# Attention maps and output rows of a two-layer decoder turned by transposing transfers instead of TensorE

## The chip, the cores and the metric

The kernel runs on one core of a Trainium2 chip. TensorE multiplies matrices, VectorE and ScalarE work on whole tiles, GpSimd does a few small steps, and SyncE issues most of the transfers; ScalarE issues some too. The metric is the device time of one execution in microseconds (us), the median over several runs. A profile comes from one execution taken by the hardware profiler.

## The reference

A sequence of 512 tokens, with 16 learned meta tokens put ahead of it, goes through two layers at width 1024. The first is gated linear attention. The second is differential softmax attention, and it is the one that matters here:

```python
proj = xn @ w_in                                  # 1024 x 8192
q, k, v, z = jnp.split(proj, 4, axis=-1)          # 8 heads; q and k have two halves p of 128
s = jnp.einsum('bhpqd,bhpkd->bhpqk', qb, kh) * scale + bias[None, :, None]
s = jnp.where(dist >= 0, s, -jnp.inf)
p = jax.nn.softmax(s, axis=-1)
a = p[:, :, 0] - lam * p[:, :, 1]                 # the map of a head
o = jnp.einsum('bhqk,bhkv->bhqv', a, vh)          # v has 256 columns a head
o = head_rms(o) * gnorm * (1.0 - lambda_init)
y = jax.nn.silu(z) * o
h = h + y @ w_out                                 # 2048 x 1024
```

All of it is fp32. A head has 4 blocks of 128 queries; block b sees the meta tokens and b + 1 blocks of 128 keys. At the end comes an RMS norm of the 512 rows.

## The kernel before, in words

Every fp32 operand of a product is split into a high part, rounded to TensorE's fast fp32 format, and a low remainder (`split`: ScalarE writes the high part, L276, VectorE the low one, L277). A product is then three passes, high by high, high by low, low by high (`mm3`, L400; `product`, L431, inside a Strassen-like scheme with seven products called `Unit`; `project`, L421). Weights come in pieces of 1 MB into two buffers called `raw`, by SyncE (L285 and L298), and are split just ahead of their use: `a11`, `a12`, `a22`, `sum` and `wh`/`wl` are the operands that a `Unit` makes of a piece.

The order of TensorE is written out by hand (a manual schedule). ScalarE, VectorE, GpSimd and SyncE get theirs from a scheduler that goes by priorities and its own estimates of durations; a function marked `urgent` gets a higher priority. Transposing transfers keep the order in which the program issues them. All engines run their lists strictly in order.

A planner, the `Weaver`, lays the list of TensorE. It holds a queue of generators, which are the projections of the next head (`q_diff_z`, `q_diff_v`, `q_diff_k`, `q_diff_q`) and the output projections of earlier heads (`q_diff_out2`). `fill(us)` takes products from the queue for so many microseconds; `finish` empties it, `follow` sets a step to be laid after so many microseconds of filling, and `land` lays all such steps at once. `behind` holds steps that are issued on SyncE just after the next load of weights.

A head of the second layer has four steps for each block, from block 3 down to block 0, laid between stretches of filling (`diff_steps`, L1663):

- A, `scores`: the products of q and k (on TensorE, L400 into `ps`), the bias added and the minimum found by VectorE (L1680), the exponentials by ScalarE (L1682), and the map a from both halves by VectorE (L1685 to L1687).
- B, `turn`: TensorE turns the map, one 128x128 transpose for each block of keys (L1695) and one for the last 32 columns, where the meta tokens are (L1696). ScalarE and VectorE split it from PSUM into `aT` and `am`.
- C, `values`: the products of the turned map and v (L400, L1711). ScalarE takes the squares (L1716), GpSimd the power -1/2 (L1718), and ScalarE copies the scaled rows to `on` (L1719).
- E, `rows`: TensorE turns `on` with two transposes (L1725), VectorE multiplies by the gate z into `yt` (L1728), and the two splits go to the output operand `hT`.

The steps of a head are laid as A3 A2 B3 A1 C3 B2 E3 A0 C2 B1 E2 C1 B0 E1 C0 E0 (the digit is the block). After A0, SyncE loads the next head's bias tile `T` (`bias_tile`, L1543), for which VectorE must have read the old one.

v of heads 1 to 6 is already turned by transfers (`turn_by_dma`): ScalarE copies the two 16-bit halves of each word apart (`planes`, L589), sends them to device memory (`vd`, L590), SyncE brings them back with transposing transfers (L598, and L600 for the last 128 columns, `lands`), and `landed` splits the result (L575, L576).

The output projection of a pair of heads (0 and 1, 2 and 3, 4 and 5) is laid as a whole among the steps of heads 2, 4 and 6; its sums are added into `hacc`. Heads 6 and 7 are projected at the end (`final_rows`).

## Time and profile before

| | us |
|---|---|
| median of 3 runs | 972.53 (971.72 to 973.37) |
| span of the profiled execution | 970.2 |
| TensorE busy | 957.1 (99%) |
| VectorE busy | 778.4 (80%) |
| ScalarE busy | 628.0 (65%) |
| GpSimd busy | 50.6 (5%) |
| DMA traffic | 104.94 MB in 128521 packets, mean 108 GB/s |

The profiled execution is 2.3 us shorter than the median. The heads of the second layer run from about 500 to 940 us of the span. In rows of the timeline the columns are start, length, engine, line, operation, the tile written and the tiles read, and the shape; in brackets stands the idle time before it and what ended it. A row with x4 stands for four instructions. "SPq" and "ACTq" are the issues of transfers by SyncE and ScalarE: their length is how long the issue holds the queue, not how long the data travels. In rows that group instructions, the total busy time is followed by the mean of one in ns, and then by the idle time before them.

### The profile page before, as it was taken

What the parts mean: (1) busy time and instruction counts of PE and PEld (TensorE: products, weight loads), DVE (VectorE), ACT (ScalarE), POOL (GpSimd) and SP (SyncE); (2) the same over time, 40 slices, a digit from 0 to 9 for tenths busy, and PEclk for the clock granted to TensorE, in tenths of its full rate; (3) what the DMA queues carried; (4) which work ended last, traced back from release to release, by engine and by line L of the source; (5) the groups of instructions that cost most, each with busy time, mean ns of one, the idle gap of its engine ahead of it and who ended that gap; (6) DMA issues with size and microseconds to landing.
All of it is one profiled execution on the core that took longest, in us unless ns stands there. A gap on an engine that the chain in (4) does not pass through costs nothing. (4 is left out here: it accounts for less than half of the span.)

```text
span 970.2 us, 18065 instructions
## 1 busy us (share of the span) xinstructions
PE 957.1 (99%) x6993; PEld 906.5 (93%) x6993; DVE 778.4 (80%) x1586; ACT 628.0 (65%) x1304; POOL 50.6 (5%) x68
## 2 busy tenths in 40 slices
PE   8999999999999999999999999999999999999997
PEld 8999999999999999898899998898998999989996
DVE  7989885886888887568997985977958879677785
ACT  7776755577647567656757774576764677655583
POOL 1000000000000100000001001001010000000001
PEclk9999999999999999999999999999999999999999
DMA  7322223635363245224355525135252352412212
GB/s 197 88 86 60 79 81 122 148 99 129 120 156 96 79 121 154 62 92 151 100 132 147 131 78 153 51 97 140 86 148 88 99 138 86 148 61 84 87 66 87
DMA packets 128521, 104.94 MB, mean 108 GB/s; under 512 B 51101, under 2 KB 112829, under 8 KB 128432
## 3 DMA queue, kind: packets, MB, share of 16 engines
q1 hardware_dynamic: 123104, 93.80, 35.1%
q10 hardware_dynamic: 5328, 9.95, 2.8%
q8 instruction: 56, 0.92, 0.4%
q14 instruction: 33, 0.27, 0.1%
HBM read 83.64 MB, written 11.80 MB: 98 GB/s over the span
## 5 line engine op out<-in xcount | busy, mean ns | idle before, releaser
L277 DVE TENSOR_TENSOR wl<-raw,wh 128x1024 fp32r<-128x1024 f32 x98 | 119.5, 1222 | 24.8 <-ACT wh L276 16.8
L276 ACT ACTIVATE wh<-raw 128x1024 fp32r<-128x1024 f32 x98 | 103.2, 1055 | 52.6 <-PE by L968 23.2
L431 PE MATMUL bv<-x,wh 128*128 128x264 f32 (+1 forms) x656 | 97.6, 286 | 0.0
L431 PE MATMUL bx<-x,wh 128*128 128x264 f32 (+1 forms) x640 | 94.9, 286 | 0.7 <-ACT u L452 0.6
L431 PEld LDWEIGHTS bv<-x,wh 128*128 128x128 f32 x656 | 86.5, 188 | 0.6 <-DVE z L479 0.3
L431 PEld LDWEIGHTS bx<-x,wh 128*128 128x128 f32 x640 | 84.5, 188 | 1.9 <-ACT u L452 1.2
L452 ACT ACTIVATE u<-bx 128x264 f32<-128x264 f32 (+1 forms) x120 | 45.4, 380 | 32.3 <-PE bx L431 31.1
L421 PE MATMUL bx<-x,wh 128*128 128x512 f32 (+1 forms) x256 | 62.4, 386 | 0.0
L277 DVE TENSOR_TENSOR wl<-sum,wh 128x1024 fp32r<-128x1024 f32 x41 | 50.1, 1221 | 14.3 <-ACT wh L276 13.9
L431 PE MATMUL bv<-x,wl 128*128 128x264 f32 (+1 forms) x328 | 55.2, 285 | 0.1
L1718 POOL TENSOR_TENSOR st<-st,mhalf 128x1 f32<-128x1 f32 x32 | 31.0, 970 | 464.4 <-ACT on L1716 408.9
L431 PE MATMUL bx<-x,wl 128*128 128x264 f32 (+1 forms) x320 | 53.9, 285 | 0.0
L1682 ACT ACTIVATE p<-p,st 128x528 f32<-128x528 f32 (+3 forms) x64 | 36.5, 571 | 25.4 <-DVE st L1680 24.9
L421 PEld LDWEIGHTS bx<-x,wh 128*128 128x128 f32 x256 | 44.5, 188 | 7.9
L276 ACT ACTIVATE wh<-sum 128x1024 fp32r<-128x1024 f32 x41 | 43.3, 1056 | 13.0 <-PE bv L431 4.0
L431 PE MATMUL by<-x,a12h 128*128 128x264 f32 (+1 forms) x320 | 46.5, 285 | 0.2 <-ACT t L1646 0.2
L431 PE MATMUL bx<-x,a11h 128*128 128x264 f32 (+1 forms) x320 | 46.3, 285 | 0.0
L431 PEld LDWEIGHTS bv<-x,wl 128*128 128x128 f32 x328 | 45.9, 188 | 0.4 <-issue 0.3
L431 PEld LDWEIGHTS bx<-x,wl 128*128 128x128 f32 x320 | 45.2, 188 | 0.6 <-DVE wl L277 0.2
L276 ACT ACTIVATE a11h<-raw 128x512 fp32r<-128x512 f32 x41 | 25.7, 627 | 28.6 <-DMA raw<-in_diff_w_in_dram 14.2
L431 PEld LDWEIGHTS bx<-x,a11h 128*128 128x128 f32 x320 | 42.2, 188 | 0.7
L431 PEld LDWEIGHTS by<-x,a12h 128*128 128x128 f32 x320 | 41.8, 188 | 0.4 <-ACT t L1646 0.4
(475 smaller groups left out, 2632.2 us busy)
## 6 DMA issues: line engine op xcount, KB each, us to landing
raw<-in_gla_w_in_dram SPq DMA_DIRECT2D x48, 512.0 KB, 4.5
raw<-in_diff_w_in_dram SPq DMA_DIRECT2D x42, 512.0 KB, 4.8
raw<-in_diff_w_in_dram SPq DMA_DIRECT2D x11, 1024.0 KB, 6.3
raw<-in_gla_w_out_dram SPq DMA_DIRECT2D x8, 1024.0 KB, 5.7
raw<-in_diff_w_out_dram SPq DMA_DIRECT2D x8, 1024.0 KB, 6.4
vd<-planes ACTq DMA_DIRECT2D x12, 268.0 KB, 7.1
vd<-keep ACTq DMA_DIRECT2D x12, 264.0 KB, 2.3
T<-bdr SPq DMA_DIRECT2D x8, 264.0 KB, 5.0
```

Of the source, the lines that this page charges most:

```text
L276: act.activation(hi, src, AF.Copy)
L277: dve.tensor_tensor(lo, src, hi.bitcast(F32), op=ALU.subtract)
L421: pe.matmul(bank, a[:, k, :], b[k] if n0 is None else b[k][:, n0 + i * nn:n0 + (i + 1) * nn], start=n == 0 and ks[0] == 0, stop=n == len(t ...
L431: pe.matmul(bank[:, :x[q].shape[2]], w[p][:, k * P:(k + 1) * P], x[q][:, k, :], start=first and i == 0, stop=i == len(PASSES) - 1, skip_gr ...
L452: W.moved = act.activation(t, self.bx[:, :self.n], AF.Copy, scale=self.sc)
L1682: act.activation(p[:, :nk], p[:, :nk], AF.Exp, scale=-1.0, bias=st[:, m:m + 1], accum_out=st[:, 2 + m:3 + m])
L1718: pool.tensor_tensor(ms, ms, mhalf[:, :1], op=ALU.pow)
```

## The change

The maps of heads 0 to 6, all four blocks, are turned by transfers: ScalarE copies the 16-bit halves of the map apart (L1704 of the new kernel) and sends them to device memory (`ad`, L1706); SyncE brings them back with two transposing transfers a block, one for the blocks of keys into `p0` to `p3` and one for the last 128 columns into `e1` to `e3`, or `keep` for block 0 (L1716); `landed` splits them into `aT` (L575). Head 7 keeps the transposes on TensorE.

The output rows of heads 2 to 6 go the same way, once for the whole head: ScalarE copies each block's `on` apart into `yt` (L1757) and sends it to `ye` (L1760); after the last block one transposing transfer brings all four back (L1765), VectorE multiplies by z in one instruction (L1770), and one split of 1024 columns follows. Heads 0, 1 and 7 keep `rows` on TensorE (L1783).

The steps of heads 0 to 6 become A3 A2 A1 A0 B3 C3 B2 E3 C2 B1 E2 C1 B0 E1 C0 E0, with 4 us of filling after each A. The two halves of an output projection are spread: one of the pair 0 and 1 to head 2, the other to head 3, then one to head 4 and one to head 5 for the next pair, and both of the third pair in head 6. The filling is divided by new shares. Steps carry tags, and `land` is called for one tag where its result is needed: "v", "y" with the head, "a" with the block. The transposing transfers of v are issued directly and no longer behind a load of weights. `tri` and `hacc` move to other pools.

Counted over the whole program, TensorE loses 138 transposes (80 to 10 of L1695, 32 to 4 of L1696, 64 to 24 of L1725) and keeps all other products. ScalarE gains 28 copies of maps, 20 copies of rows and 48 issues; SyncE gains 61 transposing transfers, 28 and 28 for the maps and 5 for the rows.

```diff
@@ turn_by_dma
-                W.follow((4.0, turn if direct else lambda: behind.append((turn, None))))
+                W.follow((4.0 if tag is None else 9.0, turn if direct else lambda: behind.append((turn, tag))), tag=tag)
@@ gate
         if s.z is None:
+            W.land(("y", heads.index(s) - 2))
@@ turned_back2: last
             split3(s.vm, pm, 32, short[:, NM + 1:NM + 2])
+            for back, take, tag in pending:
+                W.follow((0.1, back), (9.0, take), tag=tag)
+            pending.clear()
@@ turned_back2
             if m:
+                W.land("y")
                 s.leave = turn_by_dma(T(ep, [P, 2, 536], F32, "planes", bufs=1),
-                                      [(slice(3, 1, -1), 0), (slice(1, None, -1), 272)], 240, 0.0 if heads.index(s) % 2 else 11.0, done, last)
+                                      [(slice(3, 1, -1), 0), (slice(1, None, -1), 272)], 240, 9.0, done, last, True, "v")
@@ diff_steps: scores
+        by_pe, rows_by_pe = hd == D_HEADS - 1, hd in (0, 1, D_HEADS - 1)
...
+            if by_pe:
+                act.activation(r.p, r.a, AF.Copy)
+            else:
+                pl = words(r.p).rearrange("p (h c) -> p h c", h=2)
+                act.activation(pl, words(r.a).rearrange("p (c h) -> p h c", h=2), AF.Copy)
+                r.dr = T(dp, [P, 2, L], U16, "ad", bufs=4)
+                act.dma_start(r.dr[:, :, :nk], pl)
+                W.follow((9.0, lambda: back(r)), tag=("a", b))
             return r
+
+        def back(r):
+
+            w = (r.b + 1) * P
+            rows = r.dr.rearrange("p h c -> (p h) c")
+            r.ends = (T(ep, [P, P], F32, f"e{r.b}", bufs=1) if r.b else keep2[:, 4 * D:]).rearrange("p (j c) -> p j c", c=P)
+            for o, c0, c1 in ((r.p[:, :w].rearrange("p (j c) -> p j c", c=P), 0, w), (r.ends, r.nk - P, r.nk)):
+                tc.keep_in_program_order(sp.dma_start(words(o), rows[:, c0:c1], transpose=True))
@@ diff_steps: turn
+            if not by_pe:
+                W.land(("a", r.b))
...
+            else:
+                landed(hi, lo, r.p[:, :w], ticked())
+                with tc.issue_after(W.split.ins):
+                    split3(r.am, r.ends[96:, 0, :], 64)
@@ diff_steps: values
             act.activation(r.on, po, AF.Copy, scale=ms)
+            if not rows_by_pe:
+                pl = words(T(ep, [P, 256], F32, "yt", bufs=1)).rearrange("p (h c) -> p h c", h=2)
+                act.activation(pl, words(r.on).rearrange("p (c h) -> p h c", h=2), AF.Copy)
+                if s.rows is None:
+                    s.rows = T(dp, [4, P, 2, 256], U16, "ye", bufs=3)
+                act.dma_start(s.rows[b], pl)
+
+        def rows_back():
+
+            s.y = T(ep, [P, 2, NR], F32, "planes", bufs=1)
+            tc.keep_in_program_order(sp.dma_start(words(s.y), s.rows.rearrange("b p h c -> (b p h) c"), transpose=True))
+
+        @urgent
+        def rows_landed():
+            with tc.issue_after(W.mark.ins):
+                dve.tensor_tensor(s.y, s.y, s.z, op=ALU.mult)
+            split(*ys[hd], s.y)
@@ the loop over heads
+        if hd in (2, 3, 5):
+            q_diff_out2(pair, ys[pair:pair + 2], [hd % 2])
+        if hd == D_HEADS - 2:
+            q_diff_out2(pair, ys[pair:pair + 2], range(2))
...
+        if hd == 4:
+            q_diff_out2(pair, ys[pair:pair + 2], [0])
...
-        steps = [(A, 0), (A, 1), (B, 0), (A, 2), (C, 0), (B, 1), (E, 0), (A, 3), (C, 1), (B, 2), (E, 1), (C, 2), (B, 3),
-                 (E, 2), (C, 3), (E, 3)]
+            steps = [(A, 0), (A, 1), (A, 2), (A, 3), (B, 0), (C, 0), (B, 1), (E, 0), (C, 1), (B, 2), (E, 1), (C, 2), (B, 3), (E, 2), (C, 3), (E, 3)]
...
-        share = {A: 1.5, B: 1.1, C: 1.1, E: 0.5}
+        share = {A: 1.5, B: 1.1, C: 1.1, E: 0.5} if last else {B: 1.6, C: 1.0, E: 0.3 if hd < 2 else 0.0}
+        W.land("v")
```

The change moves instructions on every engine. Three places are shown. In each row stand the line, the operation, the tile written and the tiles read (a number in a name is a running one), and the shape.

SyncE in head 0, from the load of the next bias tile T. Before:

```order
L1543 DMA T_9437<-bdr_1019 128x528
L298 DMA raw_9683<-in_diff_w_in_dram 128x4x256 x2
L598 DMA_TRANSPOSE planes_9383<-vd_9384 128x2x512 x2
L600 DMA_TRANSPOSE lands_9688<-vd_9384 128x1x512
L298 DMA raw_9690<-in_diff_w_in_dram 128x4x256 x2
L298 DMA raw_9718<-in_diff_w_in_dram 128x4x256 x2
```

Now (the names with `ad` are the map's halves in device memory):

```order
L1549 DMA T_9342<-bdr_1019 128x528
L1716 DMA_TRANSPOSE p_1600_9145<-ad_9163 128x3x256
L1716 DMA_TRANSPOSE e_1644_9350<-ad_9163 128x1x256
L1716 DMA_TRANSPOSE p_1617_9237<-ad_9255 128x2x256
L1716 DMA_TRANSPOSE e_1657_9424<-ad_9255 128x1x256
L1716 DMA_TRANSPOSE p_1638_9322<-ad_9340 128x1x256
L1716 DMA_TRANSPOSE keep_8187<-ad_9340 128x1x256
L298 DMA raw_9705<-in_diff_w_in_dram 128x4x256 x2
L605 DMA_TRANSPOSE planes_9373<-vd_9374 128x2x512 x2
L607 DMA_TRANSPOSE lands_9591<-vd_9374 128x1x512
```

Six transposing transfers of the head's maps now stand between T and the next load of weights, and v's transposes have moved behind the first of these loads.

ScalarE in head 0, where the first split of the weights loaded behind T stands (a11h). `ps` is a bank of PSUM with a block's values, `on` the scaled rows (L1716 and L1719 before, L1751 and L1754 now), `am` the meta columns of a map, `u` a partial sum of a `Unit`. Before, with block 2's rows:

```order
L1715 ACTIVATE ps_9466<-st_9125 128x1
L1716 ACTIVATE on_9477,st_9125<-ps_9466 128x257
L1719 ACTIVATE on_9477<-ps_9466,st_9125 128x256
L452 ACTIVATE u_9498<-bx_9339 128x264
L276 ACTIVATE aT_1675_9524<-ps_9518 128x256
L407 ACTIVATE am_9523<-ps_9519 32x128
L408 ACTIVATE am_9523<-ps_9519 32x128
L276 ACTIVATE a11h_9693<-raw_9683 128x512
```

Now, with block 3's rows:

```order
L408 ACTIVATE am_9408<-e_1624_9266 32x128
L276 ACTIVATE wh_9461<-raw_9209 128x1024
L276 ACTIVATE a11h_9711<-raw_9705 128x512
L575 ACTIVATE aT_1665_9478<-p_1600_9145,tick_9480 128x384
L1750 ACTIVATE ps_9442<-st_9059 128x1
L407 ACTIVATE am_9477<-e_1644_9350 32x128
L1751 ACTIVATE on_9456,st_9059<-ps_9442 128x257
L408 ACTIVATE am_9477<-e_1644_9350 32x128
L1754 ACTIVATE on_9456<-ps_9442,st_9059 128x256
```

The split a11h stood behind the rows of block 2; now it stands ahead of the split of block 2's map and of both steps of `on` of block 3.

SyncE in head 1, from the load of the next bias tile. Before:

```order
L1543 DMA T_10139<-bdr_1019 128x528
L285 DMA raw_10402<-in_diff_w_out_dram 128x4x512
L598 DMA_TRANSPOSE planes_10098<-vd_10099 128x2x512 x2
L600 DMA_TRANSPOSE lands_10406<-vd_10099 128x1x512
L285 DMA raw_10408<-in_diff_w_out_dram 128x4x512
L298 DMA raw_10418<-in_diff_w_in_dram 128x4x256 x2
```

Now:

```order
L1549 DMA T_10067<-bdr_1019 128x528
L1716 DMA_TRANSPOSE p_1747_9873<-ad_9891 128x3x256
L1716 DMA_TRANSPOSE e_1789_10075<-ad_9891 128x1x256
L605 DMA_TRANSPOSE planes_9913<-vd_9914 128x2x512 x2
L607 DMA_TRANSPOSE lands_10115<-vd_9914 128x1x512
L1716 DMA_TRANSPOSE p_1765_9965<-ad_9983 128x2x256
L1716 DMA_TRANSPOSE e_1802_10152<-ad_9983 128x1x256
L298 DMA raw_10429<-in_diff_w_in_dram 128x4x256 x2
```

And ScalarE there, now:

```order
L1750 ACTIVATE ps_10170<-st_9787 128x1
L407 ACTIVATE am_10205<-e_1789_10075 32x128
L1751 ACTIVATE on_10184,st_9787<-ps_10170 128x257
L408 ACTIVATE am_10205<-e_1789_10075 32x128
L276 ACTIVATE a11h_10434<-raw_10429 128x512
L452 ACTIVATE u_10215<-bx_10042 128x264
L1754 ACTIVATE on_10184<-ps_10170,st_9787 128x256
```

Seven transposes stand behind T, v's three among them, and the split a11h of the weights loaded behind them is ahead of the copy u and of the last step of `on`. On TensorE, in heads 0 and 1 alike, 57 products of the projections, block 3's values (12 products and the one with `am`) and 30 more products of the projections stand between the last score product and the two transposes of block 3's rows (L1783).

More of the change, by code (lines that the diff above doesn't have):

```diff
@@ L576, in landed, with ticked, turn_by_dma @@
         dve.tensor_tensor(lo, src, hi.bitcast(F32), op=ALU.subtract)
-    def turn_by_dma(planes, groups, ends, us, done, last, direct=False):
+    def ticked():
+        one = T(mp, [P, 1], F32, "tick", bufs=2)
+        tc.add_manual_dep(dve.memset(one, 1.0).ins, W.mark.ins.name, mybir.DependencyInfo(
+            mybir.DependencyClass.NoSync, mybir.DependencyReason.DATA), reason="place")
+        return one
+    def turn_by_dma(planes, groups, ends, us, done, last, direct=False, tag=None):
         n = planes.shape[2]
@@ L656, in trunk @@
         sp.dma_start(wup[r:r + 1], g_b)
-    tri = cp.tile([P, P], F32, name="tri")
+    tri = T(gp, [P, P], F32, "tri")
     sp.dma_start(tri, c_tri)
@@ L1877, in trunk @@
                 W.fill(2.0)
-            if n == 4:
-                W.land()
-            if n == 5 and gates[hd] in W.queue:
+            if last and n == 5 and gates[hd] in W.queue:
                 W.finish(gates[hd])
@@ L1893, in trunk @@
                     heads[hd + 1].T = bias_tile(hd + 1)
[L1894 to L1895 removed]
+            if last:
+                W.fill(max((W.left - keep) * share[f] / sum(share[g] for g, _ in steps[n:]), 3.0 if n == len(steps) - 2 else 2.4 if f is C else 0.0))
+            elif f is A:
+                W.fill(4.0)
+            else:
+                W.fill((W.left - keep) * share[f] / (sum(share[g] for g, _ in steps[n:]) or 1.0))
     W.finish()
@@ L1898, in trunk @@
     ws.pump()
+    W.land()
     F3 = final_rows(3, wt, ys[-2:])
```

113 lines of the change are left out of this document (62 added, 51 removed).

## The prediction

> **What bounds the kernel now.** I read four views, in this order: the busy times of the page, the same by stages (the windows), TensorE's waits, and then the timelines of the queues that the change loads. First the page's first part, then the windows of the second layer, whose columns are length, PE, PEld, DVE, ACT, POOL, granted clock, DMA share, GB/s:
>
> ```profile
> PE 957.1 (99%) x6993; PEld 906.5 (93%) x6993; DVE 778.4 (80%) x1586; ACT 628.0 (65%) x1304; POOL 50.6 (5%) x68
> ```
>
> ```profile
> 500.00:920.00 420.00, 419.08 (x2883) 389.52 (x2882) 334.61 (x746) 271.39 (x624) 28.84 (x28) 1.00 0.40 110
> 531.00:540.00 9.00, 9.00 (x64) 8.27 (x63) 6.13 (x15) 6.10 (x17) 0.76 (x2) 1.00 0.92 191
> ```
>
> TensorE works 419.1 of the 420 us in which the heads run, at full granted clock. VectorE has 80%, ScalarE 65%, the DMA engines 40%, though for nine microseconds 92%: there a head's v is turned by transposing transfers while weights arrive. TensorE's waits between 500 and 960 us are these, with the total, the count and the longest of each:
>
> ```profile
> PE bx L431 <- ACT u L452: 0.6, 2, 0.4
> PE ps L400 <- DVE yt L1728: 0.2, 1, 0.2
> ```
>
> So TensorE sets the time, its order is written by hand, and nothing stops it. Two things follow. Every instruction taken off it is worth its full slot, and every microsecond by which an operand comes late is lost in full, because there was no waiting before that could absorb it.
>
> **What is removed.** The groups of transposes on TensorE (busy us, mean ns; a mean includes the pipeline), and one place where they lie between products:
>
> ```profile
> L1695 PE MATMUL ps<-ident,p 128*128 128x128 f32 x80 | 13.9, 272 | 0.0
> L1696 PE MATMUL ps<-ident,p 128*32 128x128 f32 x32 | 8.7, 272 | 0.0
> L1725 PE MATMUL ps<-ident,on 128*128 128x128 f32 x64 | 12.2, 272 | 0.0
> ```
>
> ```profile
> 509.11 0.60 PE L1695 MATMUL ps<-ident,p 128*128 128x128 f32 x4
> 509.55 0.27 PE L1696 MATMUL ps<-ident,p 128*32 128x128 f32 x1
> 509.58 1.20 PE L431 MATMUL bv<-x,wh 128*128 128x256 f32 x8
> ...
> 516.23 1.59 PE L400 MATMUL ps<-v,aT 128*128 128x256 f32 x12
> 517.66 0.28 PE L1711 MATMUL ps<-vm,am 96*128 96x256 f32 x1
> 517.78 1.13 PE L431 MATMUL bx<-x,wh 128*128 128x264 f32 x8
> 518.75 0.65 PE L431 MATMUL bx<-x,wl 128*128 128x264 f32 x4
> ```
>
> The slot of one is start to start, not the mean: four take 0.44 us (509.11 to 509.55), 0.11 each. By the same reading a product of 264 columns takes 0.97/8 = 0.12, a values product 1.43/12 = 0.12. Seven heads lose 10 + 4 transposes each (98), five lose 8 each (40): 138 x 0.109 = **15.0 us off TensorE**. No other product is added or dropped.
>
> **What is added, and where it lies.** ScalarE copies the map's 16-bit halves apart and sends them off, and SyncE turns them on the way back. The same work is already done for v, so the prices are known:
>
> ```profile
> L589 ACT ACTIVATE planes<-t x12: 1082/1084/1100, 524.1 to 831.6; 128x1072 uint16<-128x1072 uint16 x12
> L590 ACTq DMA_DIRECT2D vd<-planes x12: 338/339/397, 525.2 to 832.7; - x12
> L598 SPq DMA_TRANSPOSE planes<-vd x12: 1237/1287/4332, 531.1 to 837.5; - x12
> L575 ACT ACTIVATE v<-planes,tick x12: 708/712/728, 549.9 to 870.7; 128x512 fp32r<-128x512 f32 x12
> L576 DVE TENSOR_TENSOR v<-planes,v x12: 674/684/693, 551.8 to 873.9; 128x512 fp32r<-128x512 f32 x12
> ...
> DMA to landing us min/median/max: 5.9/7.1/8.2
> ```
>
> ```profile
> L600 SPq DMA_TRANSPOSE lands<-vd x12: 1147/1252/2052, 172.1 to 840.8; - x12
> ```
>
> ScalarE: 2688 elements of copies a head at 1.084 us per 1072, seven times, is some 20 us with their fixed parts; the output rows' 20 copies of 512 some 12 (between 0.5 and 0.71 each); 48 sends at 0.339 are 16.3; dearer splits of landed maps and fewer of rows cancel. Together about 48 us: 271 + 48 = 319 of 420, or 76%. That is no bound in itself. VectorE stays near 80%.
>
> SyncE: 61 more transposing transfers. One of 256 KB holds its queue for 1.287 us (L598) and one of 128 KB for 1.252 (L600), so I take **1.25 us each, small or large**: 76 us in all, some 11 a head, and in one bunch. It hides as long as nothing urgent stands behind it in the queue. In the order it does: after a head's last scores the load of the next bias tile T is followed by six to ten transposes, and only then by the next weights.
>
> [...]
>
> **Where the queue bites.** These rows time the chain before (start, length):
>
> ```profile
> 526.20 0.35 SPq L1543 DMA_DIRECT2D T<-bdr  x1
> 530.13 0.92 SPq L298 DMA_DIRECT2D raw<-in_diff_w_in_dram  x2
> 531.15 5.32 SPq L598 DMA_TRANSPOSE planes<-vd  x2
> ```
>
> ```profile
> 524.30 0.79 PE L400 MATMUL ps<-k,q 128*128 128x144 f32 x6
> 524.92 1.19 PE L431 MATMUL bx<-x,wh 128*128 128x264 f32 x8
> ```
>
> ```profile
> 520.57 0.47 ACT L1719 ACTIVATE on<-ps,st 128x256 f32<-128x256 f32 x1 [1.91 <-POOL st L1718]
> ...
> 527.70 0.19 ACT L1682 ACTIVATION_READ_ACCUMULATOR p<-p,st 128x1 f32 x1
> ...
> 533.84 0.63 ACT L276 ACTIVATE a11h<-raw 128x512 fp32r<-128x512 f32 x1 [0.38 <-DMA raw<-in_diff_w_in_dram]
> ```
>
> T goes 1.3 us after the end of the last score products (524.92 to 526.20), since VectorE must have read the old tile. Weights are split 3.7 us after they are asked for (530.13 to 533.84). Before, that load stood right behind T and ScalarE's split of it, a11h, came after the copy `on` that TensorE needs for the output rows. In the new order the load is behind the transposes and a11h is ahead of `on`. All times below count from the end of a head's last score products.
>
> The small steps on ScalarE and VectorE, by form:
>
> ```profile
> L1716 ACT ACTIVATE on<-ps 128x257 f32<-128x257 f32 x32 | 12.4, 386 | 0.9
> L1716 ACT ACTIVATION_READ_ACCUMULATOR on<-ps 128x1 f32 x32 | 6.2, 195 | 0.0
> L452 ACT ACTIVATE u<-bx 128x264 f32<-128x264 f32 x42 | 15.8, 380 | 5.0 <-PE bx L431 4.9
> L276 ACT ACTIVATE hT<-yt 128x256 fp32r<-128x256 f32 x32 | 13.2, 411 | 17.1 <-DVE yt L1728 13.0 <-DVE tick L612 3.7
> L276 ACT ACTIVATE aT<-ps 128x384 fp32r<-128x384 f32 x8 | 3.9, 488 | 0.3 <-PE ps L1695 0.3
> ```
>
> ```profile
> L1686 DVE SCALAR_TENSOR_TENSOR st<-st,lam 128x1 f32<-128x1 f32 x32 | 6.9, 216 | 0.5
> L1685 DVE RECIPROCAL st<-st 128x1 f32<-128x1 f32 x32 | 5.0, 158 | 7.7 <-ACT p L1682 7.7
> L1687 DVE SCALAR_TENSOR_TENSOR p<-p,st,p 128x144 f32<-128x144 f32 x8 | 3.0, 369 | 0.3
> ```
>
> Head 0. Block 0's exps end 3.0 us on (at 527.89), plus 0.74 on VectorE (the three rows), a copy of 288 elements (0.41, as for 256) and 0.34 for the send: 4.5. Its write lands 2.3 to 7.1 us later (page, sixth part):
>
> ```profile
> vd<-planes ACTq DMA_DIRECT2D x12, 268.0 KB, 7.1
> vd<-keep ACTq DMA_DIRECT2D x12, 264.0 KB, 2.3
> ```
>
> Then two transposes, 2.5: the load goes at 9.3 to 14.1 (the queue alone, 1.3 + 0.35 + 6 x 1.25, says 9.1). Add 3.7 to land, 0.63 for a11h, then what now waits behind a11h: the split of the next map 0.5, the square 0.6, GpSimd's power with its wait 1.9 and the copy 0.47. `on` is there at 17.1 to 21.9. TensorE's list reaches the rows after 87 products of 264 columns and one values block: 87 x 0.122 + 12 x 0.118 + 0.1 = 12.2. It stands **4.9 to 9.7 us; I take 6.0**, nearer the low end, since block 0 is only 72 KB.
>
> Head 1. Seven transposes behind T (v's three among them), load at 1.3 + 0.35 + 8.75 = 10.4, split done 14.7, a copy u 0.38 and `on` 0.47: 15.6 against 12.1 in the list: **3.5 us**. If the queue's time went with the bytes it would be 0.2; if v's pair holds it 5.32 instead of 2.57, as in the row above, 6.3.
>
> Heads 2 to 6 have no rows turned on TensorE, so `on` costs it nothing. There a late a11h holds back u and the next map's split. Head 2: nine transposes, load at 12.9 to 14.1, a11h done 17.2 to 18.4, the split of block 1 (0.4 and 0.4) 18.1 to 19.3; the list wants it at 18.5: 0 to 1, I take 1. Heads 3 to 6 have the same pattern with the output rows' transposes added: 0 to 2 each, I take 2.5 in all.
>
> Sum on the profiled execution: 970.2 - 15.0 + 6.0 + 3.5 + 1.0 + 2.5 = 968.2. That execution is 2.3 us under the median of the runs, so **970.5 us**. With the low ends (5 lost) it is 962.5, with the high ends (25 lost) 982.5.
>
> What I cost at nothing: v's transfer issued directly, `tri` and `hacc` in other places, the output projection's halves on other heads (the same products). If their landing points are wrong, a head's projection waits; no row prices it, and I leave it within the bounds.
>
> **Rivals.** *Hidden.* The stalls stay under 5 us, because small transposes free the queue quickly or writes land in 2.3 us. For it: the pairs of 64 KB have no row here; only 1 us of waiting in 460 shows how well the old order fitted. Against: 128 and 256 KB cost the same. Time: 972.5 - 15.0 = 957.5 with nothing lost, to 962.5.
>
> *The maps come late in every head (slower).* Block 3's scores end 23.5 us of listed products, at the slots above, before its values. The chain: reads, exps and combination 3.7 as for block 0, copy 1.1, send 0.3, write 7.1 and transposes 8.2 at their slowest so far, split 0.71 + 0.68 = 1.4: 21.8. So 1.7 us are spare, and it decides once write and transposes together pass 17.0 us. For it: the DMA share of 0.92 in the window of v's transposes, and 61 more of them. If both are 1.25 times that, 3.8 us more, TensorE stands 2.1 us in each of seven heads: 14.7 on top of the forecast, 985.2. Against: the mean share is 0.40, and median landings leave room. [...]
>
> *It doesn't do what it says.* The counts of transposes do fall in the order, so this is only that other stalls appear: no chance of its own.
>
> **How the numbers follow.** The forecast (5 to 20 lost, 962.5 to 978) gets 0.48, hidden 0.25, maps late in every head 0.2, and 0.07 stays for what I don't see. About 0.2%, 970.6 to 974.5, is what a measurement can't tell from no change. The forecast lies half below that (0.24), three tenths within (0.14) and two tenths above (0.10); of the unseen I give 0.01 to no change and 0.06 to slower. So faster 0.24 + 0.25 = 0.49, same 0.15, slower 0.10 + 0.20 + 0.06 = 0.36. The range for 8 in 10 runs from 959 to 985.
>
> **What would show it.** TensorE 138 instructions and some 15 busy us less, at a share of about 97%. Its waits would name `on` (through L1783) in heads 0 and 1, and ScalarE's a11h would wait longer than 14 us in all on its weights. SyncE's 64 KB transposes would last about 1.2 us each. If those last under 0.7 us, or a11h is there before the values, the hidden case holds; if TensorE waits at L400 for aT in every head, the maps are late. Waits at the output projection would show a term that I left out.

## The result, and the profile after

| | before | after |
|---|---|---|
| median of the runs, us | 972.86 (971.72 to 973.37, 4 runs) | 1013.07 (1012.17 to 1017.66, 4 runs) |
| span of the profiled execution | 970.2 | 1010.4 |
| TensorE: busy, instructions | 957.1, 6993 | 959.8, 6855 |

The change makes the kernel slower: ratio 1.0425, 95% interval 1.0402 to 1.0448. The prediction was 970.5 us with a range of 959 to 985.

The page's first part after the change:

```profile
PE 959.8 (95%) x6855; PEld 902.2 (89%) x6855; DVE 778.9 (77%) x1584; ACT 664.2 (66%) x1341; POOL 46.9 (5%) x68
```

The 138 instructions are gone from TensorE as forecast, but its idle time, span less busy time, went from 13.1 to 50.6 us, and its busy time rose by 2.7. Those two make up the 40.2 us between the spans. That fewer instructions take more busy time is explained further down by the clock.

TensorE's waits after the change (total, times, longest; before there were two rows with 0.8 us in the same part):

```profile
PE ps L1783 <- ACT on L1754: 9.5, 8, 2.2
PE ps L400 <- ACT aT L575: 7.9, 2, 5.8
PE bv L431 <- DVE tick L581: 6.6, 1, 6.6
PE bx L431 <- ACT u L452: 5.4, 7, 1.2
PE bx L431 <- DVE wl L277: 2.9, 1, 2.9
```

Three kinds stand out: the output rows wait for `on`, the values wait for a turned map `aT`, and projections wait for VectorE or ScalarE to empty a PSUM bank. The prediction had named the first and, as the slow rival, the second.

Head 0 shows all of it. First TensorE (start, length; the wait in brackets), then SyncE and ScalarE in the same stretch:

```profile
517.64 0.79 PE L400 MATMUL ps<-k,q 128*128 128x144 f32 x6
518.27 0.81 PE L431 MATMUL bx<-x,a11h 128*128 128x264 f32 x5
...
524.79 0.65 PE L431 MATMUL bv<-x,wl 128*128 128x264 f32 x4
531.24 3.23 PE L400 MATMUL ps<-v,aT 128*128 128x256 f32 x12 [5.80 <-ACT aT L575]
...
540.73 0.44 PE L1783 MATMUL ps<-ident,on 128*128 128x128 f32 x2 [1.06 <-ACT on L1754]
```

```profile
515.29 5.61 SPq L1421 DMA_TRANSPOSE keep<-hd  x1
521.00 2.17 SPq L1716 DMA_TRANSPOSE p<-ad  x1
523.22 1.24 SPq L1716 DMA_TRANSPOSE e<-ad  x1
524.56 0.52 SPq L1549 DMA_DIRECT2D T<-bdr  x1
525.18 1.23 SPq L1716 DMA_TRANSPOSE p<-ad  x1
...
531.62 1.24 SPq L1716 DMA_TRANSPOSE keep<-ad  x1
532.95 1.08 SPq L298 DMA_DIRECT2D raw<-in_diff_w_in_dram  x2
```

```profile
525.67 0.37 ACT L452 ACTIVATE u<-bx 128x264 f32<-128x264 f32 x1
529.43 0.94 ACTq L597 DMA_DIRECT2D vd<-planes  x2
530.47 0.72 ACT L575 ACTIVATE aT<-p,tick 128x512 fp32r<-128x512 f32 x1 [4.43 <-issue]
...
536.99 0.63 ACT L276 ACTIVATE a11h<-raw 128x512 fp32r<-128x512 f32 x1 [4.05 <-DMA raw<-in_diff_w_in_dram]
...
540.20 0.47 ACT L1754 ACTIVATE on<-ps,st 128x256 f32<-128x256 f32 x1 [0.87 <-POOL st L1753]
```

The weights are asked for 14.7 us after the last score product (518.27 to 532.95), behind eight transposes of the maps, and a11h and `on` follow as predicted. What the prediction did not have is the stop ahead of it. From 526.0 to 529.43 ScalarE does nothing: it stands on the send of v. This is what the trace has on the transfers around it. Each transfer in it counts up a semaphore when it lands, and the same eight numbers (100, 102 to 104, 107 to 110) serve all 148 transfers of SyncE and 61 of ScalarE that are issued after 500 us:

```
issued   queue    transfer    semaphore  waits for semaphore  landed
525.18   SyncE    p<-ad       108        105                  529.35
526.46   SyncE    e<-ad       109                             530.15
529.43   ScalarE  vd<-planes  108        108 (by an instruction of its own at 529.37)
```

The send of v was given semaphore 108, whose last user was a transposing transfer of SyncE, and it went when that one had landed. The two have no data in common. Behind the send stood the split of block 3's map, whose transfer had landed at 525.93, and TensorE stood for that.

After this stop TensorE ran slower, and so it did after others. Windows of the same trace (length, then busy us and instructions of PE, PEld, DVE, ACT, POOL, then the granted clock, DMA share, GB/s):

```profile
531.30:537.40 6.10, 6.10 (x27) 5.87 (x28) 2.12 (x3) 2.00 (x4) 0.00 (x0) 0.50 0.82 246
...
592.20:595.50 3.30, 3.30 (x17) 3.30 (x17) 2.50 (x5) 2.65 (x7) 0.00 (x0) 0.50 1.07 165
...
669.00:674.00 5.00, 5.00 (x18) 4.54 (x19) 4.63 (x12) 4.54 (x10) 0.91 (x1) 0.50 0.08 28
674.10:680.00 5.90, 5.90 (x32) 5.00 (x32) 3.33 (x8) 4.68 (x13) 0.55 (x1) 1.00 0.02 8
```

After the stop of head 0 the granted clock is 0.50 and TensorE does 27 instructions in 6.10 us. Block 3's twelve values products take 3.03 us there (531.24 to 534.27), 0.25 each; nine of block 2, after the clock has risen, take 1.06 (541.74 to 542.80), 0.12 each. In the second layer the clock record has five such stretches ahead of the end, from 530.70, 592.14, 667.23, 834.49 and 964.19 us, three of 6.83 and two of 3.41 us, 27.3 us together. 24.3 of them fall on work, which costs 12.1 us. Before the change there is none until 968.22 of 970.2 us. The stops that the five go with are 6.09, 2.40, 6.92, 2.00 and 3.17 us long, from the start of one instruction to the start of the next; the last section has stops in the same range with no half clock behind them.

So the account on the profiled executions is: 15.0 us of transposes off; stops in the second layer that lengthen the distance from one instruction's start to the next by 42.5 us in all (gaps of 0.5 us and more, less 0.15 each for the instruction), where the kernel before has 0.5; 12.1 us of half clock. 970.2 - 15.0 + 42.5 - 0.5 + 12.1 = 1009.3, against a span of 1010.4.

### The profile page after: what moved, and what is told of

Its sections match the earlier page's. It is cut to its first block, busy times and chain, and to the rows that moved or that the text cites. A ratio compares the mean times of both kernels' runs of the same rounds, so it can differ in the third digit from the quotient of the medians.

```text
span 1010.4 us, 18091 instructions
## 1 busy us (share of the span) xinstructions
PE 959.8 (95%) x6855; PEld 902.2 (89%) x6855; DVE 778.9 (77%) x1584; ACT 664.2 (66%) x1341; POOL 46.9 (5%) x68
## 5 line engine op out<-in xcount | busy, mean ns | idle before, releaser
L431 PEld LDWEIGHTS bx<-x,wh 128*128 128x128 f32 x640 | 85.8, 192 | 9.8 <-ACT u L452 7.4
L277 DVE TENSOR_TENSOR wl<-sum,wh 128x1024 fp32r<-128x1024 f32 x41 | 50.0, 1221 | 12.2 <-ACT wh L276 11.8
L421 PEld LDWEIGHTS bx<-x,wh 128*128 128x128 f32 x256 | 45.5, 191 | 8.5
L1753 POOL TENSOR_TENSOR st<-st,mhalf 128x1 f32<-128x1 f32 x32 | 27.4, 856 | 507.8 <-ACT on L1751 292.2
L276 ACT ACTIVATE a11h<-raw 128x512 fp32r<-128x512 f32 x41 | 25.8, 628 | 36.0 <-DMA raw<-in_diff_w_in_dram 22.3
L400 PE MATMUL ps<-v,aT 128*128 128x256 f32 x240 | 38.2, 302 | 8.3 <-ACT aT L575 7.9
L400 PEld LDWEIGHTS ps<-v,aT 128*128 128x128 f32 x240 | 35.3, 207 | 11.7 <-ACT aT L575 8.9
L366 DVE TENSOR_TENSOR sum<-raw 128x512 f32<-128x512 f32 x41 | 28.2, 688 | 20.3 <-DMA raw<-in_diff_w_in_dram 15.1
```

What stands on the lines that cost most here:

```text
L276: act.activation(hi, src, AF.Copy)
L277: dve.tensor_tensor(lo, src, hi.bitcast(F32), op=ALU.subtract)
L366: dve.tensor_tensor(o, a, b, op=ALU.add)
L400: pe.matmul(ps, l, r, start=first and n == 0, stop=last and n == 2, **kw)
L421: pe.matmul(bank, a[:, k, :], b[k] if n0 is None else b[k][:, n0 + i * nn:n0 + (i + 1) * nn], start=n == 0 and ks[0] == 0, stop=n == len(t ...
L431: pe.matmul(bank[:, :x[q].shape[2]], w[p][:, k * P:(k + 1) * P], x[q][:, k, :], start=first and i == 0, stop=i == len(PASSES) - 1, skip_gr ...
```

## The experiments

Every kernel was compared with the kernel before on the same chip (972.0 to 972.4 us there). In e1, e3 and e5 the rows of heads 2 and up are turned at once, while the second half of a pair's output projection is computed a head later; it then reads rows that the next head has overwritten, with the same instructions. e7, e12 and e13 leave out the meta tokens' part, as their expectations say.

### The new order of the steps, without any new transfer

e1 turns everything by TensorE again:

```diff
-        by_pe, rows_by_pe = hd == D_HEADS - 1, hd in (0, 1, D_HEADS - 1)
+        by_pe, rows_by_pe = True, True
```

> The change with every map and every row turned by TensorE again, so that only the new order of the steps (all scores of a head first), the spread output projection and v's transfers issued directly are left. Theory (queues): the time is lost because transposing transfers hold up weights on SyncE and sends and splits on ScalarE, and each stall of over 2 us is followed by 3.4 or 6.8 us at half clock; with no new transfers that is gone, so 971 to 978 us, no half clock before the last heads. Rival (order): the new order itself leaves TensorE without operands; then 990 us or more.

Measured: 989.53 us, ratio 1.0180 (1.0159 to 1.0201). That is next to the rival's 990: without any new transfer, and with the same products on TensorE as before, the new order and what goes with it cost 17 us. There is no half clock in the second layer ahead of its end; the mean granted clock is 0.997, against 0.986 in the change and 0.999 before. Its largest wait:

```profile
PE ps L1783 <- ACT on L1754: 10.1, 8, 1.7
```

Before, at least 2.4 us of projections were laid after a block's values, and 3.0 to 5.2 us between the last block's values and its rows. The change dropped these minima with the line that held them. e5 is e1 with them:

```diff
-                W.fill((W.left - keep) * share[f] / (sum(share[g] for g, _ in steps[n:]) or 1.0))
+                W.fill(max((W.left - keep) * share[f] / (sum(share[g] for g, _ in steps[n:]) or 1.0),
+                           (4.0, 3.0, 5.2, 3.0, 4.6, 3.0, 4.0, 3.0)[hd] if n == len(steps) - 2 else 2.4 if f is C else 0.0))
```

> As the run with everything turned by TensorE in the new order (989.5 us, 17 over before), but with the smallest fillings of before put back: at least 2.4 us of projections after each block's values, and 3.0 to 5.2 us between the last block's values and its rows. Theory (minima): the loss of the order is that the rows of a block follow its values so closely that ScalarE's and GpSimd's chain to `on` can't be done; 10.1 of 13.8 us of TensorE's waits name it, so 974 to 981 us. Rival (scores first): the order A A A A itself starves TensorE; then 986 or more.

Measured: 981.26 us, ratio 1.0091 (1.0074 to 1.0107). The minima bring 8.3 of the 17 us back and the row for `on` shrinks:

```profile
PE bx L431 <- ACT u L452: 2.8, 3, 1.7
PE ps L1783 <- ACT on L1754: 1.2, 1, 1.2
```

The theory was right for half. The other 9 us come with what else e5 shares with the change: the order itself, the moved output projection, v's transfers issued directly, and in e1 and e5 one copy of each map on ScalarE that the kernel before doesn't have (L1701, 15.3 us in all). Their waits are small and spread over many tiles, and no run separates them.

e11 puts the minima into the change, which otherwise stays as it is:

> The change with only the smallest fillings of before put back (2.4 us after the values of each block, 3.0 to 5.2 between the last block's values and its rows); all transfers stay. With everything on TensorE these minima gave 8.3 us back. If the losses add up: 1003 to 1008 us, with the waits of the rows in heads 0 and 1 down from 9.5 to about 4 us. If the stalls behind late weights take their place: 1010 to 1015.

Measured: 1002.85 us, ratio 1.0320 (1.0301 to 1.0339), 10.2 us less than the change, so the losses do about add up. The wait of L1783 falls from 9.5 to 2.4 us; the waits for `aT` grow from 7.9 to 10.2.

### Rows alone and maps alone

e2 keeps all maps on TensorE and sends the rows of heads 2 to 6; e3 does the opposite (`by_pe` or `rows_by_pe` set to True).

> All maps turned by TensorE, the output rows of heads 2 to 6 by transfers as in the change: 40 transposes fewer than before on TensorE (4.4 us), 5 transposing transfers and 20 sends more. Queues: five transfers and 20 sends lie far from the weights' loads, so 966 to 980 us. Order: 985 or more. If the rows were the main cause of the loss: over 995.

> The maps of heads 0 to 6 turned by transfers as in the change, all output rows by TensorE: 98 transposes fewer than before (10.7 us off), 56 transposing transfers and 28 sends more. Queues: nearly the whole loss stays, 1003 to 1018 us, with the same stalls in heads 0 to 2. If the rows caused it: under 985.

Measured: e2 988.26 us, ratio 1.0158 (1.0141 to 1.0175); e3 1018.05, ratio 1.0462 (1.0444 to 1.0479). Against e1 the rows are worth -1.3 us, which the noise covers, with 40 transposes (4.4 us) less, and the maps cost 28.5 us with 98 transposes (10.7 us) less. Seen from the other side, the change is 24.8 us slower than e2. So the maps lose 36 to 39 us to gain 10.7; the rows nearly pay for themselves. e2 came out where its expectation had put the order's loss, 985 or more, and not at 966 to 980.

e10 asks whether rows by transfers gain in the order before, for the heads 0, 2 and 4, whose rows are first read two heads later:

```diff
+        s.rows, by_dma = None, hd in (0, 2, 4)
...
+            elif not b:
+                W.follow((6.0, rows_back), (9.0, rows_landed), tag="y")
```

> The kernel before with its own order of steps, only the output rows of heads 0, 2 and 4 turned by transfers (as the change does for heads 2 to 6); these heads' rows are first read two heads later, so there are some 50 us for the way. 24 transposes less on TensorE, 2.6 us; three transposing transfers and 12 sends more. Queues: nothing urgent stands behind them, 968.5 to 971.5 us, a gain. Rival: any transposing transfer among the loads costs a stall of 1 us or more: 972 to 978.

Measured: 972.74 us, ratio 1.0007 (0.9998 to 1.0016). No difference; the 2.6 us went to waits:

```profile
PE bx L431 <- ACT u L452: 1.5, 1, 1.5
PE bx L431 <- ACT wh L276: 0.6, 1, 0.6
PE ps L400 <- ACT aT L276: 0.5, 1, 0.5
```

Neither side was right. In an order in which TensorE has no slack, even a dozen sends and three transposes with plenty of time push something else late. No version here beats the kernel before.

### The transposes in SyncE's queue

e4 sends only blocks 3 and 2 of the maps:

```diff
-        by_pe, rows_by_pe = hd == D_HEADS - 1, hd in (0, 1, D_HEADS - 1)
+        on_pe, rows_by_pe = lambda b: hd == D_HEADS - 1 or b < 2, hd in (0, 1, D_HEADS - 1)
```

> Only blocks 3 and 2 of the maps of heads 0 to 6 go by transfers, blocks 1 and 0 are turned by TensorE; rows as in the change. SyncE has 28 transposes fewer than in the change, and behind T stand two instead of six in head 0, five instead of seven in head 1, five instead of nine in head 2. Queues: the split a11h comes 5 us earlier in heads 0 and 2, most of the long stalls and half-clock stretches go, 978 to 995 us. Rival (traffic): what slows the kernel is the small packets of the transposes on the DMA engines; blocks 1 and 0 are 3 of 10 key blocks and half of the 64 KB pieces, so about a third of the loss goes, 1000 us or more.

Measured: 1000.18 us, ratio 1.0275 (1.0254 to 1.0296), 12.9 less than the change: half of the maps' 24.8 us. That lies between the two expectations (at the border of traffic's 1000), so it did not tell them apart. e7 drops the 64 KB transposes:

```diff
-            for o, c0, c1 in ((r.p[:, :w].rearrange("p (j c) -> p j c", c=P), 0, w), (r.ends, r.nk - P, r.nk)):
+            for o, c0, c1 in ((r.p[:, :w].rearrange("p (j c) -> p j c", c=P), 0, w),):
```

> The change without the 28 transposing transfers of 64 KB (the last 128 columns of each map, which carry the meta columns); `am` is split from other rows of the map in their place, so the meta tokens' part of the output is left out. Queues: SyncE has 35 us less to issue, the load behind T goes 2.5 to 5 us earlier in heads 0 to 2, so a third to two thirds of the maps' loss goes: 988 to 1003 us. Traffic: these are 1.8 of 8.3 MB that the new transposes move, so about a fifth of the maps' 25 us: 1006 to 1010.

Measured: 997.80 us, ratio 1.0278 (1.0257 to 1.0298), 15.3 us less than the change. That took both queue time and data away. e13 puts an ordinary 64 KB transfer in the place of each, e14 issues each transpose twice:

```diff
 e13
+                if c0:
+                    tc.keep_in_program_order(sp.dma_start(r.ends[:, 0, :], d_w_in[:P, r.b * P:r.b * P + P]))
 e14
+                for _ in range(2 if c0 else 1):
+                    tc.keep_in_program_order(sp.dma_start(words(o), rows[:, c0:c1], transpose=True))
```

> The change with each of the 28 transposing transfers of 64 KB replaced by an ordinary transfer of 64 KB (of weights, so the meta tokens' part of the output is left out), at the same place of the order of SyncE. It tells the time that a transposing transfer holds SyncE's queue (1.24 us) from the bytes that it moves. Queue time: an ordinary transfer should hold the queue for 0.35 us, so nearly all of the 15 us that leaving them out gave: 998 to 1003 us. Traffic: the same bytes, so little: 1008 to 1014.

> The change with each of the 28 transposing transfers of 64 KB issued twice (the result is the same): 35 us more on SyncE's queue, 2.5 to 5 us more between T and the weights of each head. Queue time: about as much more as leaving them out gave less, 1022 to 1032 us. If the queue had slack there: under 1018.

Measured: e13 1005.55 us, ratio 1.0342 (1.0323 to 1.0360); e14 1049.21, ratio 1.0797 (1.0777 to 1.0817). What one issue holds of SyncE's queue, in the change and in e13 (ns, least, median, most), with the time to landing:

```profile
L1716 SPq DMA_TRANSPOSE e<-ad x21: 1227/1238/1791, 523.2 to 910.1; - x21
...
DMA to landing us min/median/max: 3.0/3.1/3.2
```

```profile
L1717 SPq DMA_DIRECT2D e<-in_diff_w_in_dram x21: 564/572/837, 523.2 to 902.5; - x21
...
DMA to landing us min/median/max: 2.8/3.5/4.1
```

The kernels differ in how long the 28 issues hold the queue, and the weights of head 0 are asked for earlier or later; these are the rows of e7, e13 and e14 (the change has 532.95):

```profile
527.74 1.08 SPq L298 DMA_DIRECT2D raw<-in_diff_w_in_dram  x2
```

```profile
530.09 1.11 SPq L298 DMA_DIRECT2D raw<-in_diff_w_in_dram  x2
```

```profile
534.41 1.08 SPq L298 DMA_DIRECT2D raw<-in_diff_w_in_dram  x2
```

| | queue time against the change, us | time against the change, us |
|---|---|---|
| e7, none | -34.7 (28 x 1.24) | -15.3 |
| e13, ordinary, same size | -18.6 (28 x (1.238 - 0.572)) | -7.5 |
| e14, twice | +34.4 (28 x 1.227) | +36.1 |

The time follows the queue, some 0.4 us for each microsecond taken away and 1.05 for each added. With the same bytes moved, e13 still gains half of e7's 15 us, about in proportion to the queue time that it takes away. It lies between its two ranges, since an ordinary issue holds the queue 0.57 us and not 0.35; e14 went above its range. In e14 the added issues don't only make the load later. The scheduler put 6, 8 and 9 transposes between T and the load in heads 0 to 2 (6, 7 and 9 in the change) and the others behind it, so the load goes 0.8 to 1.3 us later after T, and by which ways the 36 us arise was not followed.

That the bytes on the DMA engines are the main cause does not fit: e13 would have stayed at 1008 or more, and the weights take 4.6 us to land in the change and 4.8 before. What a transposing transfer may ask of the DMA engines beyond its bytes is not told apart from its queue time by these runs. The landing lines above rest on the two of 21 pieces that the view could follow. By the semaphores, all 21 took 2.4 to 9.0 us in the change, 4.5 in the median, and the ordinary ones of e13 2.1 to 9.3, 3.8 in the median; slow ones stand together, as the three of the change from 901.56 to 910.06 with 4.7 to 6.0. In head 1 a map's transpose that was issued at 577.45, beside 1 MB of weights and the sends of v, landed at 588.76. TensorE stood 2.4 us for this map, most of it because ScalarE, which splits it, stood until 589.21 on the send of another map and then did a step of z.

### What stands behind the late weights

The longest stop in heads 1 to 6 of the change is in head 2. Its weights are asked for at 661.92, 13.5 us after T and behind nine transposes. Before the change the next load of weights there went 2.1 us after T, with no transpose between. These are the rows of the change:

```profile
665.70 0.63 ACT L276 ACTIVATE a11h<-raw 128x512 fp32r<-128x512 f32 x1 [7.44 <-DMA raw<-in_diff_w_in_dram]
666.36 0.69 DVE L277 TENSOR_TENSOR a11l<-raw,a11h 128x512 fp32r<-128x512 f32 x1 [7.14 <-ACT a11h L276]
...
668.46 0.42 DVE L477 SCALAR_TENSOR_TENSOR t<-bv,u 128x264 f32<-128x264 f32 x1
668.94 2.13 PE L431 MATMUL bv<-x,wh 128*128 128x264 f32 x8 [6.63 <-DVE tick L581]
```

ScalarE and VectorE both stand for the weights, and only then comes the step `t` that reads the bank `bv`, which TensorE wants next. (`tick` is a small step of VectorE that ends at the same time.) With an earlier load this wait shrinks, to 4.7 us in e13 and 2.2 in e7.

e6 moves the split a11h on ScalarE behind the copy `on` of block 2:

```diff
-                with tc.issue_after(W.moved.ins) if calm and b == 0 else ExitStack():
+                at = W.moved if calm else W.on
+                with tc.issue_after(at.ins) if at is not None and b == 0 else ExitStack():
```

> The change, with the split a11h of the weights tied behind the copy `on` of block 2 on ScalarE, so that it doesn't stand ahead of `on` and of the splits of maps in heads 0 to 2; all transfers stay. Queues: the waits of 6.9 us in head 2 and of 2.4 and 1.3 for the first rows in heads 1 and 0 go, and with them 3 to 7 us of half clock: 996 to 1005 us. Rival (traffic): the weights and maps land late whatever waits for them, 1008 or more.

Measured: 1018.33 us, ratio 1.0479 (1.0462 to 1.0497): not faster. In head 2 TensorE stands for 6.7 us as it did. The reason, on VectorE and on ScalarE there:

```profile
667.05 0.69 DVE L367 TENSOR_TENSOR sum<-raw 128x512 f32<-128x512 f32 x1 [8.02 <-DMA raw<-in_diff_w_in_dram]
```

```profile
667.04 0.63 ACT L276 ACTIVATE a12h<-raw 128x512 fp32r<-128x512 f32 x1 [8.31 <-DMA raw<-in_diff_w_in_dram]
```

The same late weights have several readers. With a11h out of the way, a12h stood first on ScalarE, and VectorE stood on the sum, ahead of what empties TensorE's banks. So it does not matter which of the readers stands first in a queue, as long as the load is late. The rival's number came true, and its statement that the weights are late whatever waits for them; that traffic makes them late is what e13 speaks against.

e9 takes the sends off ScalarE:

```diff
-                act.dma_start(r.dr[:, :, :nk], pl)
+                pool.dma_start(r.dr[:, :, :nk], pl)
```

and likewise for v of the second layer and for the rows.

> The change with the sends of the second layer (maps, v of heads 1 to 6, output rows) issued by GpSimd, which is 95% idle, in place of ScalarE. In the change ScalarE stood 3.7 us in head 0 on the send of v, for the semaphore of a transposing transfer that has nothing to do with it, and 1.5 us in head 1 on the send of a map. Queues: those waits leave ScalarE, the 6.1 us stop of TensorE in head 0 shrinks to about 2 and its 6.8 us at half clock go, the 2.4 us in head 1 goes too: 998 to 1006 us. Rival: the maps land late by themselves, and who issues the send makes no difference: 1010 to 1016. If GpSimd's issues are slow and its power for `on` waits behind them: above 1016.

Measured: 1015.98 us, ratio 1.0450 (1.0434 to 1.0466), no gain. Yet the stop in head 0 did shrink as expected, from 5.80 to 1.28 us:

```profile
526.42 0.50 PE L400 MATMUL ps<-v,aT 128*128 128x256 f32 x2 [1.28 <-ACT aT L575]
...
540.20 0.69 PE L1783 MATMUL ps<-ident,on 128*128 128x128 f32 x2 [6.32 <-ACT on L1754]
```

The rows that follow stood 6.32 instead of 1.06 us, and went at 540.20 instead of 540.73. The weights are asked for at 532.92, where they were asked for in the change, and `on` comes 7 us later. The first stop had only hidden the second. In head 1 the order of SyncE changed as well: all the map's transposes stand ahead of the load, which goes at 601.03 instead of 595.65, and the rows stand 9.7 us instead of 2.2. So e9 does not show what the sends alone are worth. Its time is that of the rival (1010 to 1016), but the first map was not late by itself.

e12 takes three things away together: the 64 KB transposes, the sends on ScalarE and the missing minima.

> The change without the 64 KB transposes (so the meta tokens' part of the output is left out), with the sends of the second layer by GpSimd and with the minima back: the three causes named so far taken away together. If each is a cause of its own: 998 for the first less 8 for the minima and 2 to 8 for the sends, 980 to 990 us, still above before, since 33 of the 61 transposes remain in front of the weights. If they only hand the stall on to the next late operand: 993 or more.

Measured: 993.68 us, ratio 1.0219 (1.0201 to 1.0236). That is 4 us under e7, where the two additions had been counted at 10 or more: they mostly hand the stall on. Its largest wait is now for VectorE:

```profile
PE bv L431 <- DVE tick L581: 15.0, 3, 5.5
```

33 of the 61 transposes are still in SyncE's queue. The remaining 21.7 us above the kernel before, 9 of which come without any new transfer (e5), are not taken apart further.

### The clock by itself

e8 is the kernel before with a split on ScalarE repeated in four heads, so that TensorE stands once in each:

```diff
+            if b == 3:
+                for _ in range({2: 12, 3: 16, 4: 20, 5: 24}.get(hd, 0)):
+                    act.activation(r.aT[0][:, :w], pt[:, :w], AF.Copy)
```

> The kernel before, with ScalarE's split of block 3's map repeated 12, 16, 20 and 24 times more in heads 2 to 5 (0.52 us each; the result is the same), so that TensorE waits once in each of four heads: about 2, 4, 6 and 8 us after some 4 us of slack. Theory (clock): a wait of over about 2.4 us brings 3.4 or 6.8 us at half clock behind it, 1.7 or 3.4 us of loss on top of each wait: 998 to 1006 us. Rival: the half clock has another cause and comes with no wait here; then the added time is the waits alone, about 993, and the granted clock stays at 1.00.

Measured: 1019.69 us in one run; the profiled span is 1017.9. The stops were 1.8 and 1.0 in a row, 9.2, 7.2 and 14.8 us, longer than expected, so the time missed its range, and the clock fell behind every one (0.976 in the mean of the span):

```profile
708.95:713.30 4.35, 4.35 (x19) 4.12 (x20) 0.65 (x1) 0.87 (x4) 0.09 (x1) 0.50 0.31 110
713.50:718.00 4.50, 4.50 (x39) 4.49 (x39) 2.50 (x4) 2.61 (x8) 0.26 (x1) 1.00 0.01 4
...
778.85:785.00 6.15, 6.15 (x27) 5.92 (x28) 1.42 (x3) 1.65 (x5) 0.55 (x1) 0.50 0.00 0
```

19 instructions in 4.35 us at 0.50 and 39 in 4.50 us at 1.00. No other cause is in this kernel, which is the one before apart from the repeated splits. The stops make 36.6 us and the half clock some 11.5; together 48.1, against 47.7 between the spans.

## Why the prediction was wrong

**What is removed: right.** 138 instructions are off TensorE, and nothing was added there.

**The price of a transpose in the queue: right for the small ones, too low in the sum.** "1.25 us each, small or large": the 64 KB pieces, of which the trace before had none, take 1.238. But the pieces of 256 KB (block 3) held the queue for 1.25 to 2.49 us and the five of the output rows for 3.21 to 5.56, so all 61 took 97.5 us and not 76. An ordinary transfer of the same 64 KB (e13) was cheaper: 0.57 us against 1.24 in the queue, and 3.8 against 4.5 from issue to landing, in the median.

**Head 0: the place right, the size too small.** The prediction put `on` at 17.1 to 21.9 us after the last score product; it came 22.4 after it (518.27 to 540.67), and the list wanted it at 12.2. The lateness was 10 us, of which 6.0 were forecast. Three terms were off. The load of T went 6.3 us after the scores, not 1.3, since the queue ahead of it held `keep` and two transposes of block 3, which the sum began behind. The split of block 3's map waited for an unrelated transfer's semaphore. And the rows of blocks 2, 1 and 0 stopped too (0.8 to 1.6 us each), because the fillings between values and rows were gone.

**Heads 1 to 6: the failed step.** "There a late a11h holds back u and the next map's split" with "0 to 1, I take 1" for head 2, and 2.5 for heads 3 to 6. Measured by the same gaps: head 1 9.6 us for 3.5, head 2 9.4 for 1.0, the rest with the end 13.4 for 2.5. In head 2 the step counted only the reader a11h and only on ScalarE. The late weights stop VectorE as well, so that a bank is not emptied; this is the 6.6 us in head 2. In head 1 the term itself was large enough: the rows of block 3 stood 2.45 us from start to start. What the sum did not have there are a map (2.4) and the rows of blocks 2, 1 and 0 (1.4, 1.5 and 2.2). Near the end TensorE waits 2.9 us for the split wl, which stands on VectorE behind the steps of head 6's rows (L1770 and a split of 1024 columns). That wait comes only where rows go by transfers (e2, e4, the change), though not in e11 and e12.

**"What I cost at nothing": the second failed step.** v's transfer, `tri`, `hacc` and the spread output projection were left "within the bounds", and the order of the steps itself got no price at all. The dropped minima, the new order and these moves cost 17 us without a single new transfer (e1). The full difference has the removed line with the minima, and the rows quoted in the prediction show that it takes 3 us from the values of a block (end 517.94) to its `on` (end 521.04).

**The clock was not in the sum.** The prediction read the granted clock as 1.00 throughout and kept it so. With stops of several microseconds, 12.1 us were added that no term held. This alone moves the sum from 970.5 to 982.6.

**The rivals.** "Hidden" is refuted. "The maps come late in every head" had the right sign, 985.2 us, and the wrong mechanism: the 5.80 us of `aT` in head 0 come from ScalarE's queue while the map had landed, in head 1 the map was late but ScalarE's queue made up most of the stop, and heads 2 to 6 have hardly any wait for `aT`. The cost did not come from the transposes' own length on the path but from what stood behind them.

**What would show it.** The waits through L1783 and the longer wait of a11h for its weights (14.2 before, 22.3 after) came as listed. TensorE's share fell to 95% instead of 97, and its busy time rose by 2.7 us instead of falling by 15, which the list did not foresee.

## What to carry to other kernels

Where an engine is 99% busy and waits for nothing, the planned distances between its steps are the design: list every distance that an edit shortens or drops, and price it, before counting what is saved. A transfer costs its queue as well as the path of its data (here 1.24 us of SyncE's queue for 64 KB transposed, 0.57 for 64 KB as they are), so count the queue time of every new issue that stands ahead of an urgent load, and ask for each late load who all of its readers are and what stands behind each of them on every engine. A stop of TensorE can cost more than itself: the 6.83 us of half clock behind some of those here cost up to 3.4 us more, and one stop of 2.00 us was enough for 3.41 us of it.

## What the runs showed of the hardware that I had not expected

Ahead of the end of the change the half clock came in stretches of 3.41 and 6.83 us, and the stretches at full clock between them were multiples of 3.413 us too (54.61 is 16 times that, 71.68 is 21 times). A stop well under 3.41 us was enough for it: one from 831.38 to 833.38, 2.00 us, was followed by 3.41 us at half clock from 834.49, and one of 3.17 us by 6.83; stops of 2.45 and 2.24 us (598.38 and 615.55) were followed by none. So the bounds in the expectations, over 2 us in e1 and over about 2.4 us in e8, were estimates that these stops don't bear out. Counted in steps of 3.413 us from the edges of the stretches, the stop of 2.00 us fills 58% of its step and half clock followed; the long stop of head 0 fills 62% of the step up to 527.28, and the clock fell only at 530.70, after the next step. So the idle share of a step alone doesn't sort these two. Which rule decides was not shown.

A send waited 3.7 us (from the end of its copy at 525.77 to 529.43) for a transfer with which it shares only the semaphore that reports the end. The waits that the profile puts down to "issue" can hide such a case: the row of `aT` above says 4.43 us of issue, and only the list of semaphores tells that a landing ended it.

Issuing an ordinary transfer of 64 KB with 128 rows held SyncE's queue for 0.57 us, a transposing one for 1.24. A transposing transfer of 256 KB took no more at its shortest (1.25 us), but up to 2.49 in the change's bunches.
